# Both feed-forward projections of a residual block by one level of Strassen's seven block products

## The chip, the cores and the metric

The kernel runs on one core of a Trainium2 chip. The time is the device time of one execution in microseconds; the kernel before takes 2693.98 us (median of three runs, 2692.53 to 2694.37). The engines are TensorE (PE, with its weight loads as PEld), VectorE (DVE), ScalarE (ACT), GpSimd (POOL) and SyncE (SP), which issues the DMAs here.

## The reference

One residual block over 2048 rows of 1024 float32 numbers: a mixer (a gated linear recurrence beside stick-breaking attention) and a feed-forward part, which is where the change is:

```python
def rms_norm(x, g):
    xf = x.astype(jnp.float32)
    xf = xf * lax.rsqrt(jnp.mean(xf * xf, axis=-1, keepdims=True) + EPS)
    return xf.astype(x.dtype) * g
...
        x = x + jnp.einsum('bse,ed->bsd', y, w_out[l])

        h2 = rms_norm(x, norm_ffn[l])
        gu = jnp.einsum('bsd,df->bsf', h2, w_ffn_in[l])
        x = x + jnp.einsum('bsf,fd->bsd', jax.nn.silu(gu[..., :D_FF]) * gu[..., D_FF:], w_ffn_out[l])
    return rms_norm(x, norm_final)
```

D_FF is 2816, 22 tiles of 128. The two projections are 2048 x 1024 x 5632 and 2048 x 2816 x 1024.

## The kernel before

**Products in three parts.** Each float32 operand is split into a high part rounded to fp32r (an ACT cast) and the low rest (a subtraction on DVE or POOL). A product is three matmuls, high by high, high by low and low by high (`mm3`, lines 115 to 118), which add up in one PSUM bank of 128x512.

**The order.** The PE order is the order in which the program is written. The other engines' instructions are placed by a scheduler at build time, and each engine runs its list strictly in order; an instruction at the head of a list that waits holds all behind it.

**The mixer** goes through four groups (`NG`) of 512 rows. The projections of the next group, and in the last group the products with `w_out` (`Mix.run`, PSUM `po`), are fill between the steps of attention. `store_rows` writes the finished rows to DRAM (`x2_d`) and takes their norms. The products of the last group's attention branch come after all attention (`tail.run`).

**Feed-forward.** It takes two halves of 1024 rows. `make_h2` loads rows back (`hn`), scales them, transposes them on PE (`h2t`) and splits them (`hhi`, `hlo`), 16 tiles of 128x512 for a half. `gate_up` then takes one tile f of D_FF at a time: weights `gur`, 512 KB for gate (j = 0) and up (j = 1) each, split into `guh` and `gul`, and 8 steps of the contraction for two token groups into the banks `pgu`. SiLU on ACT (L829), the product with up on DVE (L830) and a split into `ahi` and `alo` keep the result on chip. After every two tiles `down` multiplies what the previous two left with `dnr`, split into `dnh` and `dnl`, into 16 banks `pw`; DVE adds each at once to the rows in SBUF (L860). So the two projections alternate all the way. At the end of a half `finish` takes the final norm: squares on ACT (L884), a product with the gain `gfin` on POOL (L888), a Newton reciprocal root of small DVE instructions, a scaling and a store.

Of the kernel before, what the change touches and what calls it, by code (L numbers as in the profile page):

```python
# [36 lines left out]
FCH = 2  # L37
# [11 lines left out]
HB = 8  # L49
# half groups of mixer weights loaded ahead, and held before their parts are kept in DRAM  # L50
# [3 lines left out]
# units of filling before the first branch's product, and fewer of them in the last group  # L54
# [3 lines left out]
# the last row tiles of the groups in which the final norm is taken  # L58
ENDS = (2, 4, 6, 7)
# [7 lines left out]
def tile_block(ctx: ExitStack, tc: tile.TileContext, x, w_in, w_out, w_gu, w_dn,  # L67
# [72 lines left out]
    def load_x(g, parts=1):  # L140
        """The normalized rows of a token group, before the gain, in pieces."""
# [40 lines left out]
    def load_half(src, name, key, keep):  # L182
        """Half (over k) of a group of weight columns, split; the parts are kept in DRAM for the next use."""
# [52 lines left out]
    def proj_col(g, cg, c, w, use, mid=None):  # L236
        """A transposed column tile of group cg; use(column tile, psum) evacuates."""
# [50 lines left out]
    # ---- attention  # L288
# [28 lines left out]
    def score(p, s):  # L317
# [10 lines left out]
        # u is what each key leaves to the older ones, 1 - beta  # L328
# [18 lines left out]
    def turn(p, s):  # L347
        """Transposes the weights of a query tile and splits them."""
# [339 lines left out]
    with tc.manual_schedule(engines={mybir.EngineType.PE}):  # L688
# [112 lines left out]
        for _ in h2:  # L801
            pass
# [173 lines left out]
```

## Time and profile before

| | |
|---|---|
| median of three runs | 2693.98 us |
| span of the profiled execution | 7685.8 us |
| matmuls and transposes in the span | 13472 |
| PE, DVE, ACT, POOL busy | 7656.3, 1421.4, 1124.6, 896.9 us |
| moved by DMA | 350.05 MB |

The profiled execution took 2.85 times as long as a run without the profiler. 2693.98 us over 13472 matmuls and transposes are 0.200 us each, 7685.8 over the same are 0.570: the profile's steps on PE can't be those of the run. What the trace shows for PE is its order and its counts. Its durations on the other engines and of transfers have nothing to do with PE's step, and are used as they stand.

### The profile page before, as it was taken

The page shows a single profiled execution, that of the slowest core. Times are in us where ns is not written, and L with a number is a line of the kernel's source. Part 1 is how long each engine was busy: PE and PEld are TensorE (multiplying, and loading weights), DVE is VectorE, ACT ScalarE, POOL GpSimd, SP SyncE. Part 2 cuts the span into 40 slices and gives each one's busy share as a digit, 9 for nine tenths or more (in the row PEclk, how much of TensorE's full clock was granted, in tenths as well). Part 3 has the DMA queues.
Part 4 walks back from the last instruction along what each step waited for, and adds up shares of the span by engine and source line. Part 5 has one row for each costly group of instructions (what it writes and reads, how often), then busy time and mean ns, then how long its engine had stood idle before and what let it go on. Part 6 is the DMA issues. An engine that isn't in the chain of part 4 may idle for free.

```text
span 7685.8 us, 36652 instructions
## 1 busy us (share of the span) xinstructions
PE 7656.3 (100%) x13472; PEld 5024.0 (65%) x13472; DVE 1421.4 (18%) x2278; ACT 1124.6 (15%) x2024; POOL 896.9 (12%) x1261
## 2 busy tenths in 40 slices
PE   9999999999999999999999999999999999999999
PEld 5665676767676888888755555555555555555555
DVE  1112222223333333333100000000011000000002
ACT  2112212222222222222100000000011000000001
POOL 2211101100001110000010111111111111111111
DMA  3222222121111222211200000000011000000000
GB/s 106 78 82 73 92 71 69 59 71 55 56 59 61 68 76 66 76 50 49 79 19 14 19 19 18 18 19 19 17 36 55 19 19 17 19 19 19 17 17 25
DMA packets 167445, 350.05 MB, mean 46 GB/s; under 512 B 17504, under 2 KB 58464, under 8 KB 167264
## 3 DMA queue, kind: packets, MB, share of 16 engines
q1 hardware_dynamic: 167264, 347.70, 13.7%
q8 instruction: 106, 1.74, 0.1%
q14 instruction: 75, 0.61, 0.0%
HBM read 268.20 MB, written 79.43 MB: 45 GB/s over the span
## 4 chain that ended last, share of the span: by engine, by line
PE 100%; DVE 0%; DMA 0%; SPq 0%; issue 0%; ACT 0%
PE pgu L116 11%; PE pgu L117 11%; PE pgu L118 11%; PE y L375 6%; PE z L325 6%; PE t L360 6%; PE pw L117 6%; PE pw L116 5%; PE pj L116 5%; PE pj L118 5%; PE pw L118 5%; PE pj L117 5%; PE po L116 3%; PE po L117 3%; PE po L118 3%; PE pv L117 1%
## 5 line engine op out<-in xcount | busy, mean ns | idle before, releaser
L116 PE MATMUL pgu<-hhi,guh 128*128 128x512 f32 x1408 | 1201.0, 853 | 0.0
L117 PE MATMUL pgu<-hlo,guh 128*128 128x512 f32 x1408 | 1200.2, 852 | 0.0
L118 PE MATMUL pgu<-hhi,gul 128*128 128x512 f32 x1408 | 1200.1, 852 | 0.0
L116 PEld LDWEIGHTS pgu<-hhi,guh 128*128 128x128 f32 x1408 | 505.8, 359 | 363.1 <-issue 361.6
L117 PEld LDWEIGHTS pgu<-hlo,guh 128*128 128x128 f32 x1408 | 505.2, 359 | 360.6 <-issue 360.6
L118 PEld LDWEIGHTS pgu<-hhi,gul 128*128 128x128 f32 x1408 | 503.7, 358 | 362.9 <-issue 358.7
L116 PE MATMUL pj<-ht_hi,w_hi 128*128 128x512 f32 x512 | 601.0, 1174 | 0.0
L117 PE MATMUL pw<-dnl,ahi 128*128 128x512 f32 x704 | 587.9, 835 | 0.0
L118 PE MATMUL pw<-dnh,alo 128*128 128x512 f32 x704 | 587.6, 835 | 0.0
L116 PE MATMUL pw<-dnh,ahi 128*128 128x512 f32 x704 | 586.5, 833 | 0.0
L118 PE MATMUL pj<-ht_hi,w_lo 128*128 128x512 f32 x512 | 559.7, 1093 | 0.0
L117 PE MATMUL pj<-ht_lo,w_hi 128*128 128x512 f32 x512 | 559.0, 1092 | 0.0
L325 PE MATMUL z<-ks,qd 128*128 128x512 f32 (+2 forms) x640 | 552.6, 998 | 0.0
L360 PE MATMUL t<-ident,be 128*128 128x128 f32 x1088 | 534.3, 690 | 0.0
L830 DVE TENSOR_TENSOR sg<-pgu,sg 128x512 f32<-128x512 f32 x88 | 60.9, 692 | 2530.6 <-PE pgu L118 2516.7
L860 DVE TENSOR_TENSOR x<-pw,x 128x512 f32<-128x512 f32 x352 | 243.4, 692 | 987.0 <-PE pw L118 987.0
L360 PEld LDWEIGHTS t<-ident,be 128*128 128x128 f32 x1088 | 270.8, 249 | 234.2 <-issue 160.4
L785 POOL TENSOR_TENSOR gul<-gur,guh 128x1024 fp32r<-128x1024 f32 x88 | 208.0, 2364 | 1729.8 <-ACT guh L784 1635.4
L375 PE MATMUL y<-al,vs 128*128 128x256 f32 x576 | 395.7, 687 | 0.0
L375 PE MATMUL y<-ah,vs 128*128 128x256 f32 x576 | 395.0, 686 | 0.0
L116 PE MATMUL po<-wo_hi,yhi 128*128 128x256 f32 x512 | 384.2, 750 | 0.0
L118 PEld LDWEIGHTS pw<-dnh,alo 128*128 128x128 f32 x704 | 249.6, 355 | 172.8 <-issue 172.4
(183 smaller groups left out, 7820.4 us busy)
## 6 DMA issues: line engine op xcount, KB each, us to landing
gur<-in_w_gu SPq DMA_DIRECT2D x88, 512.0 KB, 3.4
w_hi<-w_d SPq DMA_DIRECT2D x50, 512.0 KB, 3.3
w_lo<-w_d SPq DMA_DIRECT2D x50, 512.0 KB, 4.6
dnr<-in_w_dn SPq DMA_DIRECT2D x88, 256.0 KB, 2.6
vs<-vs_d SPq DMA_DIRECT2D x80, 256.0 KB, 3.0
ks<-ks_d SPq DMA_DIRECT2D x80, 256.0 KB, 3.0
qd<-q_d SPq DMA_DIRECT2D x128, 128.0 KB, 2.8
w_raw<-in_w_in SPq DMA_DIRECT2D x30, 512.0 KB, 4.3
```

Of the source, the lines that this page charges most:

```text
L116: nc.tensor.matmul(ps, lhsT=w_hi, rhs=m_hi, start=first, stop=False)
L117: nc.tensor.matmul(ps, lhsT=w_hi, rhs=m_lo, start=False, stop=False)
L118: nc.tensor.matmul(ps, lhsT=w_lo, rhs=m_hi, start=False, stop=last)
L325: nc.tensor.matmul(z[:, :nz], lhsT=qd[:, i, qs], rhs=kss[p.c][:, :nz], start=i == 0, stop=i == 1)
L360: nc.tensor.transpose(tp[:, b, :], p.be[s][:, b * P:(b + 1) * P], ident)
L375: nc.tensor.matmul(y, lhsT=vs[:, b, :], rhs=t[:, b].rearrange("p s q -> p (s q)"), start=first and m == 0, stop=last and m == 1)
L785: nc.gpsimd.tensor_tensor(out=wlo, in0=raw, in1=f32(whi), op=ALU.subtract)
L830: nc.vector.tensor_tensor(out=sg, in0=pss[1, g], in1=sg, op=ALU.mult)
L860: nc.vector.tensor_tensor(out=x2[t][:, ns], in0=ps, in1=x2[t][:, ns], op=ALU.add)
```

## The change

**Gate-up.** Two tiles of D_FF, two halves of the contraction and two token groups form a 2x2 by 2x2 block product, a "quad" (`quad`). It had 8 block products of 12 matmuls (4 steps of the contraction, three parts); now it has 7. Weights are combined for each quad (`prep_weights`: s1 to s4), tokens once for a half (`prep_tokens`: t1 to t4). There are 44 quads: gate, then up, for 11 pairs of tiles in each half. The result goes to DRAM (`act_d`), 11.5 MB for a half.

**Down** is a stage of its own, after all of gate-up. For each half it takes seven products one after another (0 to 6 here), and each goes through the contraction in six chunks: five of two tiles (24 matmuls), and a last one of one tile (12). `operands` makes a chunk's two operands, one chunk ahead (`bp`, two buffers): a sum or difference `sa` of results on POOL, one `sb` of weights on DVE (in place, so it bears the name `dr`), a cast of each on ACT, the low parts on DVE (`blo`, and `alo` where there is a `sa`) or POOL. Products 0 and 3 have `sa` alone, 1 and 2 `sb` alone, 4 to 6 both. At the end of a product `add` puts each of four banks into one to three places of the rows. `finish` for most of the final norm is called after product 5, the rest in product 6.

**The rows for feed-forward.** `turn_rows` scales, transposes and evacuates a finished token group and writes it to DRAM (`h2_d`); for groups 0 to 2 this is fill in the last group's attention, for group 3 it follows the last product with `w_out`. `prep_tokens` loads tiles of `h2_d` and makes the combinations.

```diff
...
+ORDER = (("a11", "b11"), ("s3", "t3"), ("s2", "t2"), ("s1", "t1"), ("a22", "t4"), ("s4", "b22"), ("a12", "b21"))
+EARLY = ("b11", "t1", "t2", "t3", "t4")
...
+DOWN = (
...
+    (((0, 0, 1), (1, 1, 1)), ((0, 0, 1), (1, 1, 1)), ((0, 0, 1), (1, 1, 1))),
+    (((1, 0, 1), (0, 0, -1)), ((0, 0, 1), (0, 1, 1)), ((1, 1, 1),)),
+    (((0, 1, 1), (1, 1, -1)), ((1, 0, 1), (1, 1, 1)), ((0, 0, 1),)),
+)
+CHUNKS = ((0, 2), (4, 2), (8, 2), (12, 2), (16, 2), (20, 1))
...
+    def turn_rows(g, x2):
...
+        for k in range(KD):
+            tp = ps_d.tile([P, GT], F32, tag="d", name=f"h2t{g}_{k}")
+            for t in range(TPG):
+                nc.tensor.transpose(tp[:, t * P:(t + 1) * P], x2[t][:, k * P:(k + 1) * P], ident)
+            ht = stg.tile([P, GT], F32, tag="s", name=f"h2{g}_{k}")
+            nc.scalar.activation(ht, tp, AF.Copy, scale=gf[:, k:k + 1])
+            nc.sync.dma_start(out=h2_d[g][k], in_=ht)
...
+            def split(q, kk, src, pool):
+                hi, lo = (t[:, kk] for t in tok[q])
+                nc.scalar.copy(hi, src)
+                (nc.gpsimd if pool else nc.vector).tensor_tensor(out=lo, in0=src, in1=f32(hi), op=ALU.subtract)
...
+                    b11, b12, b22 = load(0, 0), load(0, 1), load(1, 1)
+                    split("b11", kk, b11, True)
+                    t3 = prp.tile([P, GT], F32, tag="r", name=f"t3_{half}_{kk}")
+                    nc.vector.tensor_tensor(out=t3, in0=b22, in1=b12, op=ALU.subtract)
...
+        steps = prep_tokens(0, EARLY)
+            if i % 3 == 2:
+                next(steps, None)
+        for _ in turn_rows(NG - 1, tail_x2):
+            next(steps, None)
+        for _ in steps:
...
+            hi = wsp.tile([P, KD, P], F32R, tag="hi2", name=f"a1h{nm}", bufs=2)
+            lo = wsp.tile([P, KD, P], F32R, tag="lo2", name=f"a1l{nm}", bufs=2)
+            nc.scalar.copy(hi, r[0])
+            nc.gpsimd.tensor_tensor(out=lo, in0=r[0], in1=f32(hi), op=ALU.subtract)
+            w["a11"], w["a12"] = (hi[:, :K2], lo[:, :K2]), (hi[:, K2:], lo[:, K2:])
+            s3 = new("s3", a11, a21, ALU.subtract)
+            split("s3", s3, True)
+            s1 = new("s1", a21, a22, ALU.add)
+            s2 = new("s2", s1, a11, ALU.subtract)
+            split("s2", s2, False)
+            split("s1", s1, False)
+            split("a22", a22, True)
+            nc.vector.tensor_tensor(out=s2, in0=a12, in1=s2, op=ALU.subtract)
+            split("s4", s2, True)
...
+            product("a", 0)
+            p1 = keep("a", "p1")
+            product("c", 1)
+            product("a", 2, True)
+            u2 = keep("a", "u2")
+            u3 = tmp.tile([P, GT], F32, tag="t", name=f"u3{nm}")
+            nc.vector.tensor_tensor(out=u3, in0=ps["c"], in1=u2, op=ALU.add)
+            product("d", 3)
+            use(1, 1, ps["d"], u3)
+            product("c", 4, True)
+            use(1, 0, ps["c"], u2)
+            product("d", 5, True)
+            use(0, 1, ps["d"], u2)
+            product("b", 6)
+            use(0, 0, ps["b"], p1)
...
+            def use(i, k, ps, part):
+                c = tmp.tile([P, GT], F32, tag="c", name=f"c{half}_{fp}_{j}_{i}{k}", bufs=CB)
+                nc.vector.tensor_tensor(out=c, in0=ps, in1=part, op=ALU.add)
+                if j == 0:
+                    nc.scalar.activation(c, c, AF.Silu)
+                    gates[i, k] = c
+                else:
+                    nc.vector.tensor_tensor(out=c, in0=c, in1=gates[i, k], op=ALU.mult)
+                    nc.sync.dma_start(out=act_d[half][2 * fp + i][:, k], in_=c)
...
+                r0 = (f0 + j * m) * P
+                nc.sync.dma_start(out=t, in_=w_dn[r0:r0 + m * P, k * GT:(k + 1) * GT].rearrange("(m p) c -> p m c", p=P))
+                bb.append(t)
+            sa = aa[0]
+            if len(ta) == 2:
+                sa = bp.tile([P, m, GT], F32, tag="sa", name=f"sa{nm}")
+                nc.gpsimd.tensor_tensor(out=sa, in0=aa[0], in1=aa[1], op=ALU.add if ta[1][2] > 0 else ALU.subtract)
+            sb = bb[0]
+            if len(tb) == 2:
+                nc.vector.tensor_tensor(out=sb, in0=bb[0], in1=bb[1], op=ALU.add if tb[1][2] > 0 else ALU.subtract)
+            out = []
+            for q, src, eng in (("a", sa, nc.gpsimd if len(ta) == 1 else nc.vector), ("b", sb, nc.vector)):
+                hi = bp.tile([P, m, GT], F32R, tag=f"{q}hi", name=f"{q}hi{nm}")
+                lo = bp.tile([P, m, GT], F32R, tag=f"{q}lo", name=f"{q}lo{nm}")
+                nc.scalar.copy(hi, src)
+                eng.tensor_tensor(out=lo, in0=src, in1=f32(hi), op=ALU.subtract)
+                out.append((hi, lo))
+            return out
...
+        def add(half, p, t, ps):
+            x2 = rows(half)
+            for i, k, sign in DOWN[p][2]:
+                xs = x2[i * TPG + t][:, k * GT:(k + 1) * GT]
+                if sign > 0:
+                    nc.vector.tensor_tensor(out=xs, in0=ps, in1=xs, op=ALU.add)
+                else:
...
+                    sq = op.tile([P, GT], F32, tag="sq", name=f"sqo{half}_{t}_{c}", bufs=1)
+                    nc.scalar.activation(sq, x2[t][:, cs], AF.Square, accum_out=ss[:, t, c:c + 1])
+                    o = os[t, c] = op.tile([P, GT], F32, tag="o", name=f"o{half}_{t}_{c}")
+                    if (t, c) != (TPG - 1, 0):
+                        nc.gpsimd.tensor_tensor(out=o, in0=x2[t][:, cs], in1=gfin[:, cs], op=ALU.mult)
...
+            if last and p == len(DOWN) - 2:
+                for t in range(TPG, TPH):
+                    finish(half, t, 1, ss, os, (0, 1))
+                    if t % 2:
+                        write(half, t - 1, 2, ss, os)
+                finish(half, 0, TPG, ss, os, (1,))
```

How it shifts the engines' lists shows at five places. First DVE in gate-up of the kernel before, some 40 us of feed-forward (sg is SiLU of gate, x2 the rows, pw a bank of the down product):

```order
L830 TENSOR_TENSOR sg0_6_0_16883<-pgu0_6_1_0_16833,sg0_6_0_16883 128x512
L830 TENSOR_TENSOR sg0_6_1_16890<-pgu0_6_1_1_16858,sg0_6_1_16890 128x512
L830 TENSOR_TENSOR sg0_7_0_17009<-pgu0_7_1_0_16959,sg0_7_0_17009 128x512
L830 TENSOR_TENSOR sg0_7_1_17016<-pgu0_7_1_1_16984,sg0_7_1_17016 128x512
L860 TENSOR_TENSOR x2_0_0_15707<-pw0_4_0_0_17035,x2_0_0_15707 128x512
L860 TENSOR_TENSOR x2_0_1_15709<-pw0_4_1_0_17043,x2_0_1_15709 128x512
```

The same engine in a quad of the changed kernel (s2l and s1l are low parts of the next quad's weights, u3 a partial sum out of bank c, c the results):

```order
L862 TENSOR_TENSOR s2l0_1_0_16209<-s2s0_1_0_16206,s2h0_1_0_16208 128x512
L882 TENSOR_TENSOR s2s0_1_0_16206<-r0_1_0_0_16190,s2s0_1_0_16206 128x512
L862 TENSOR_TENSOR s1l0_1_0_16213<-s1s0_1_0_16204,s1h0_1_0_16212 128x512
L907 TENSOR_TENSOR u30_0_1_16269<-psc0_0_1_16227,u20_0_1_16267 128x512
L934 TENSOR_TENSOR c0_0_1_11_16283<-psd0_0_1_16228,u30_0_1_16269 128x512
L939 TENSOR_TENSOR c0_0_1_11_16283<-c0_0_1_11_16283,c0_0_0_11_16142 128x512
L934 TENSOR_TENSOR c0_0_1_10_16299<-psc0_0_1_16227,u20_0_1_16267 128x512
L939 TENSOR_TENSOR c0_0_1_10_16299<-c0_0_1_10_16299,c0_0_0_10_16157 128x512
```

DVE reads PSUM in every row of before; now the weight rows have both inputs in SBUF, and u3, which must be out of bank c before product 4 of the quad may add to it, stands behind s1l.

DVE at the boundary of products 4 and 5 of the down stage (names end in half_product_chunk; dr with two inputs is sb):

```order
L1002 TENSOR_TENSOR blo0_4_3_23485<-dr0_4_3_00_23473,bhi0_4_3_23484 128x1024
L996 TENSOR_TENSOR dr0_4_4_00_23512<-dr0_4_4_00_23512,dr0_4_4_11_23514 128x1024
L996 TENSOR_TENSOR dr0_4_5_00_23551<-dr0_4_5_00_23551,dr0_4_5_11_23553 128x512
L1002 TENSOR_TENSOR alo0_4_4_23520<-sa0_4_4_23516,ahi0_4_4_23519 128x1024
L1002 TENSOR_TENSOR blo0_4_4_23524<-dr0_4_4_00_23512,bhi0_4_4_23523 128x1024
L996 TENSOR_TENSOR dr0_5_0_00_23590<-dr0_5_0_00_23590,dr0_5_0_01_23592 128x1024
L1002 TENSOR_TENSOR alo0_4_5_23559<-sa0_4_5_23555,ahi0_4_5_23558 128x512
L1002 TENSOR_TENSOR blo0_4_5_23563<-dr0_4_5_00_23551,bhi0_4_5_23562 128x512
L996 TENSOR_TENSOR dr0_5_1_00_23625<-dr0_5_1_00_23625,dr0_5_1_01_23627 128x1024
L1011 TENSOR_TENSOR x2_0_0_22489<-pw0_4_0_23406,x2_0_0_22489 128x512
L1002 TENSOR_TENSOR alo0_5_0_23598<-sa0_5_0_23594,ahi0_5_0_23597 128x1024
```

The sum for chunk 5 stands ahead of the low parts of chunk 4, so it waits for its weights in front of them; and the first addition to the rows stands ahead of chunk 0's low parts of the next product.

POOL in product 6 of the first half (sa are sums of results, o the rows times the final gain):

```order
L993 TENSOR_TENSOR sa0_6_0_23828<-act0_0_22455 128x1024
L993 TENSOR_TENSOR sa0_6_1_23977<-act0_1_22472 128x1024
L1025 TENSOR_TENSOR o0_4_1_23861<-x2_0_4_22497,gfin_22453 128x512
L1025 TENSOR_TENSOR o0_5_0_23865<-x2_0_5_22499,gfin_22453 128x512
L993 TENSOR_TENSOR sa0_6_2_24020<-act0_2_22534 128x1024
L1025 TENSOR_TENSOR o0_5_1_23869<-x2_0_5_22499,gfin_22453 128x512
L1025 TENSOR_TENSOR o0_6_0_23908<-x2_0_6_22501,gfin_22453 128x512
L1025 TENSOR_TENSOR o0_6_1_23912<-x2_0_6_22501,gfin_22453 128x512
L1025 TENSOR_TENSOR o0_7_0_23916<-x2_0_7_22503,gfin_22453 128x512
L1025 TENSOR_TENSOR o0_7_1_23920<-x2_0_7_22503,gfin_22453 128x512
L993 TENSOR_TENSOR sa0_6_3_24059<-act0_3_22575 128x1024
```

Ten products o stand between the sums of chunks 1 and 5, seven of them here; the sum of chunk 3 comes after these seven.

SP where gate-up of both halves ends and down begins (c are the last results of gate-up, act and x2 the loads of down):

```order
L940 DMA act_d1_20_191<-c1_10_1_00_22424 128x512
L988 DMA dr0_0_1_00_22477<-in_w_dn 128x2x512
L973 DMA x2_0_2_22493<-x2_d0_113 128x1024
L964 DMA act0_0_22455<-act_d0_0_149 128x1024
L964 DMA act0_0_22455<-act_d0_1_150 128x1024
L964 DMA act0_0_22455<-act_d0_2_151 128x1024
L964 DMA act0_0_22455<-act_d0_3_152 128x1024
L964 DMA act0_1_22472<-act_d0_4_153 128x1024
L964 DMA act0_1_22472<-act_d0_5_154 128x1024
L964 DMA act0_1_22472<-act_d0_6_155 128x1024
L964 DMA act0_1_22472<-act_d0_7_156 128x1024
L973 DMA x2_0_3_22495<-x2_d0_113 128x1024
```

Down's loads of results stand behind the last store of gate-up; before, nothing was loaded there but weights.

## Rows read from the trace of the kernel before

**Rows 1.** Page, head and busy time of PE.

```profile
span 7685.8 us, 36652 instructions
PE 7656.3 (100%) x13472; PEld 5024.0 (65%) x13472; DVE 1421.4 (18%) x2278; ACT 1124.6 (15%) x2024; POOL 896.9 (12%) x1261
```

**Rows 2.** Page, the chain that ended last, by engine.

```profile
PE 100%; DVE 0%; DMA 0%; SPq 0%; issue 0%; ACT 0%
```

**Rows 3.** Windows: the mixer, all of feed-forward, and a stretch of it.

```profile
core 0: us, PE busy (x) PEld busy (x) DVE busy (x) ACT busy (x) POOL busy (x), PEclk, DMA share, GB/s
0.00:4000.00 4000.00, 3980.46 (x7330) 2859.25 (x7331) 1075.29 (x1694) 845.86 (x1594) 458.06 (x983) 1.00 0.21 68
4000.00:7686.00 3686.00, 3675.89 (x6143) 2164.77 (x6141) 346.08 (x584) 278.71 (x430) 438.80 (x278) 1.00 0.06 21
...
4600.00:5200.00 600.00, 600.00 (x1009) 354.55 (x1009) 53.98 (x78) 38.77 (x55) 69.25 (x44) 1.00 0.06 19
```

**Rows 4.** Lines: matmuls of gate-up and down (one of three each).

```profile
L116 PE MATMUL pgu<-hhi,guh 128*128 128x512 f32 x1408 | 1201.0, 853 | 0.0
L118 PE MATMUL pw<-dnh,alo 128*128 128x512 f32 x704 | 587.6, 835 | 0.0
```

**Rows 5.** Lines of ACT: casts, copies, evacuation, squares (busy us, mean ns).

```profile
L784 ACT CAST guh<-gur 128x1024 fp32r<-128x1024 f32 x88 | 92.0, 1047 | 1065.6 <-PE pgu L117 1063.0 <-DMA gur<-in_w_gu 2.6
L844 ACT CAST dnh<-dnr 128x512 fp32r<-128x512 f32 x88 | 54.2, 619 | 1089.6 <-PE pw L118 1089.6
L775 ACT ACTIVATE hhi<-h2t,gf 128x512 fp32r<-128x512 f32 x32 | 22.0, 687 | 53.1 <-PE h2t L774 53.1
L520 ACT COPY gx<-pj 128x512 f32<-128x512 f32 x16 | 9.4, 586 | 63.4 <-PE pj L118 63.4
```

**Rows 6.** Lines of DVE, forms apart.

```profile
L860 DVE TENSOR_TENSOR x<-pw,x 128x512 f32<-128x512 f32 x352 | 243.4, 692 | 987.0 <-PE pw L118 987.0
L776 DVE SCALAR_TENSOR_TENSOR hlo<-h2t,gf,hhi 128x512 fp32r<-128x512 f32 x32 | 24.0, 751 | 44.3 <-ACT hhi L775 44.3
L362 DVE TENSOR_TENSOR al<-t,ah 128x384 fp32r<-128x384 f32 x32 | 17.9, 558 | 128.7 <-ACT ah L361 128.7
L362 DVE TENSOR_TENSOR al<-t,ah 128x128 fp32r<-128x128 f32 x32 | 9.3, 291 | 120.0 <-ACT ah L361 120.0
```

**Rows 7.** Lines of POOL.

```profile
L785 POOL TENSOR_TENSOR gul<-gur,guh 128x1024 fp32r<-128x1024 f32 x88 | 208.0, 2364 | 1729.8 <-ACT guh L784 1635.4 <-DMA x_d<-xo 94.4
L888 POOL TENSOR_TENSOR o<-x,gfin 128x512 f32<-128x512 f32 x30 | 37.9, 1276 | 84.4 <-DVE x L860 25.4 <-PE h2t L774 21.6 <-DMA out<-o 16.9
```

**Rows 8.** DMA: KB of one, median us to landing.

```profile
w_lo<-w_d SPq DMA_DIRECT2D x50, 512.0 KB, 4.6
hn<-x_d SPq DMA_DIRECT2D x32, 256.0 KB, 3.9
```

**Rows 9.** Windows at the start, where loads queue up.

```profile
0.00:5.00 5.00, 0.00 (x0) 0.00 (x0) 0.41 (x5) 1.87 (x3) 1.41 (x14) 1.00 0.59 210
5.00:10.00 5.00, 0.00 (x0) 0.00 (x0) 2.55 (x15) 4.75 (x17) 0.00 (x0) 1.00 1.03 377
```

**Rows 10.** Timeline: DVE and POOL side by side (start us, us).

```profile
3566.96 1.31 POOL L613 TENSOR_TENSOR acc<-acc,yt 128x512 f32<-128x512 f32 x1 [8.31 <-ACT yt L612]
3567.06 2.29 DVE L339 TENSOR_TENSOR_SCAN u<-u,u,zero 128x513 f32<-128x513 f32 x1
...
3569.94 0.68 DVE L345 TENSOR_TENSOR be<-be,u 128x512 f32<-128x512 f32 x1
3569.97 1.78 POOL L613 TENSOR_TENSOR acc<-acc,yt 128x512 f32<-128x512 f32 x1 [0.46 <-ACT yt L612]
```

**Rows 11.** Lines of DVE: the same scan, mean of all.

```profile
L339 DVE TENSOR_TENSOR_SCAN u<-u,u,zero 128x513 f32<-128x513 f32 x192 | 249.9, 1302 | 501.9 <-ACT u L329 501.6 <-POOL u L327 0.2
```

**Rows 12.** The chain at the end of the span.

```profile
7675.40 0.50 PE pw L118
7675.93 0.69 DVE x L860
...
7680.68 0.72 ACT o L904
```

More of the change, by code (lines that the diff above doesn't have):

```diff
@@ L48 @@
 WB = 4
-HB = 8
+WSB = 6
+CB = 6
+OB = 8
 AHEAD = 2
@@ L85, in tile_block @@
     x2_d = [dram.tile([GT, D], F32, name=f"x2_d{i}") for i in range(NG)]
+    h2_d = [[dram.tile([P, GT], F32, name=f"h2_d{i}_{k}") for k in range(KD)] for i in range(NG)]
+    act_d = [[dram.tile([P, 2, GT], F32, name=f"act_d{i}_{f}") for f in range(NF)] for i in range(NHALF)]
     smp = ctx.enter_context(tc.tile_pool(name="smp", bufs=2))
@@ L780, in split_gu @@
-        def split_gu(raw, half, f, j):
-            nc.sync.dma_start(out=raw, in_=w_gu[f, j])
-            whi = wgu.tile([P, KD, P], F32R, tag="gu_hi", name=f"guh{half}_{f}_{j}")
-            wlo = wgu.tile([P, KD, P], F32R, tag="gu_lo", name=f"gul{half}_{f}_{j}")
-            nc.scalar.copy(whi, raw)
-            nc.gpsimd.tensor_tensor(out=wlo, in0=raw, in1=f32(whi), op=ALU.subtract)
-            return whi, wlo
-        early = {}
-        h2 = make_h2(0)
-        hs = next(h2)
-        for _ in range(KD):
-            next(h2)
+        up_r = ExitStack()
@@ new lines, in tile_block, with act, rows @@
+        acts, x2s = {}, {}
+        def act(half, c):
+            if (half, c) not in acts:
+                f0, m = CHUNKS[c]
+                t = acts[half, c] = actp.tile([P, 2 * m, 2, GT], F32, tag=f"act{c}", name=f"act{half}_{c}")
+                for i in range(2 * m):
+                    nc.sync.dma_start(out=t[:, i], in_=act_d[half][f0 + i])
+            return acts[half, c]
+        def rows(half):
+            if half not in x2s:
+                x2s[half] = []
+                for t in range(TPH):
+                    xt = x2p.tile([P, D], F32, tag=f"x2_{t}", name=f"x2_{half}_{t}")
+                    gt = half * TPH + t
+                    nc.sync.dma_start(out=xt, in_=x2_d[gt // TPG][gt % TPG * P:(gt % TPG + 1) * P, :])
+                    x2s[half].append(xt)
+            return x2s[half]
@@ new lines, in tile_block @@
+        work = [(half, p, c) for half in range(NHALF) for p in range(len(DOWN)) for c in range(len(CHUNKS))]
+        ready = operands(*work[0])
+        pss = {}
+        for n, (half, p, c) in enumerate(work):
+            (ahi, alo), (bhi, blo) = ready
+            if n + 1 < len(work):
+                ready = operands(*work[n + 1])
+            if c == 0:
+                rows(half)
+                if p == 0:
+                    ss = smp.tile([P, TPH, 2], F32, tag="sso", name=f"sso{half}", bufs=1)
+                    os = {}
+            last = c == len(CHUNKS) - 1
+            for t in range(TPG):
+                if c == 0:
+                    pss[t] = ps_w.tile([P, GT], F32, tag="w", name=f"pw{half}_{p}_{t}")
+                ts = slice(t * P, (t + 1) * P)
+                m = CHUNKS[c][1]
+                for i in range(m):
+                    mm3(pss[t], ahi[:, i, ts], alo[:, i, ts], bhi[:, i], blo[:, i],
+                        c == 0 and i == 0, last and i == m - 1)
+                if not last:
+                    continue
+                add(half, p, t, pss[t])
+                if p == len(DOWN) - 1:
+                    finish(half, t, 1, ss, os, (0,))
+                    if t >= TPG - 2:
+                        write(half, *((0, TPG - 1) if t == TPG - 2 else (t, 1)), ss, os)
+            if last and p == len(DOWN) - 2:
+                for t in range(TPG, TPH):
+                    finish(half, t, 1, ss, os, (0, 1))
+                    if t % 2:
+                        write(half, t - 1, 2, ss, os)
+                finish(half, 0, TPG, ss, os, (1,))
```

286 lines of the change are left out of this document (134 added, 152 removed), and 4 rows, old and new, of the table DOWN.

## The prediction

> **What bounds the kernel now.** I read the page's head first, then the chain, then windows. In the profiled execution PE is busy 100% of the span and the chain is PE alone [rows 1, 2]. That tells little of the run: in a stretch of feed-forward 1009 matmuls take 600 us, 0.595 us each [rows 3], and 13472 at the run's mean take 0.200. So the profile hides under PE whatever doesn't exceed 0.6 us per matmul, and PE's duration must be bounded otherwise. A matmul of 512 columns at the granted clock (1.00 in every window, the level of 2.4 GHz) takes no less than 0.213 us. From above: DVE is busy 1075 us before 4000 us [rows 3], its durations hold in the run, so the mixer takes at least 1075 us of the 2694, and the 6143 matmuls behind it at most 0.263 each. I take 0.22, near the floor, since in feed-forward no other engine comes near PE's load: DVE's 346 us, POOL's 439 and ACT's 279 [rows 3] stand against 6143 x 0.213 = 1310 us. So feed-forward is bound by PE in the run too, and fewer matmuls shorten it.
>
> The Trainium skill (TensorE: Matmul & The Clock Gate, Wait — 56ns, not 53.3ns?) gives 215.7 ns from one warm matmul of 512 columns to the next. By that the gain below would be 171 us instead of 174; no row here shows it, the profile's step is 0.595.
>
> **What goes.** Gate-up has 3 x 1408 matmuls and down 3 x 704 [rows 4], 6336 in all. After: 44 quads x 84 = 3696, and 14 products x (5 x 24 + 12) = 1848; 5544. It saves 792 x 0.22 = 174 us (169 by the floor, 208 by the ceiling).
>
> **What comes, gate-up.** A product of a quad lasts 12 x 0.22 = 2.64 us, a quad 18.5. For each quad DVE has eight instructions with both inputs in SBUF and five that read PSUM, 0.69 each [rows 6], 9.0 us; POOL 2.36 + 3 x 1.28 = 6.2 [rows 7]; ACT one cast of 1.05, five of 0.62 and two copies of 0.59 [rows 5], 5.3, and SiLU every other quad. All fit in 18.5. The tight place is u3: after the third product ACT casts s1h (0.62) and copies u2 (0.59), DVE adds u3 (0.69): 1.9 us and some hand-offs, against the 2.64 of product 3, which goes to another bank. It fits with some 0.4 us to spare, so I cost it at nothing; a rival says what it costs when the cover is gone.
>
> **What comes, around the stages.** (a) Three groups' 96 transposes, 24 evacuations and 12 row scalings lie in the last attention, where the 32 transposes of half of `make_h2` had been in the tail: 24 x 0.69 [rows 5] = 17 us of ACT beside work on PE, 0 to 10 on the path, 6 taken. (b) Group 3: after the last `po` the root, scalings, eight evacuations (5.5) and a store and load through DRAM (each some 4 us [rows 8]) stand ahead of gate-up, about 14 us where before about 8 were; 5 to 14 more, I take 8. (c) Between halves the kernel before is paced by 16 evacuations of `h2t`, 16 x 0.75 = 12 us on DVE [rows 6]. After, eight tile pairs of combinations wait for buffers that the last products hold; the ones that the first product needs take about 15 us, 23 if DVE and POOL take turns. 4 to 13 more, 8 taken. (d) From gate-up to down: SP's list puts the loads of results behind the last store, so the first product needs 0.5 (gain) + 4.2 (rows) + 11.5 (results) + 2.9 (weights) = 19.1 MB while it runs. At 377 GB/s, the highest of the rows [rows 9], that is 51 us, and some 5 more until the last chunk is prepared and multiplied: 56 where 132 x 0.22 = 29 us of work are. 27 lost; at 210 GB/s [rows 9] it is 67. (e) Between the halves of down the next results come behind the output's stores, partly under product 6: 12 us (5 to 20).
> These are 6 + 8 + 8 + 27 + 12 = 61 us, with 41 and 107 as ends.
>
> **What comes, in down's chunks.** A chunk of two tiles lasts 24 x 0.22 = 5.28 us on PE, a product 29. An operation of 128x1024 takes POOL 2.36 [rows 7], ACT 1.05 [rows 5]; for DVE no row has it, and I go on from 384 and 128 columns, 558 and 291 ns [rows 6], 134 ns for each 128: 1.23. DVE has 2.5 us in a chunk of products 0 to 3 and 3.7 in one of 4 to 6, POOL 2.36, ACT 2.1: less than 5.28. A pair of weight loads lands in 4.6 [rows 8]; with issue, sum, cast and low part, some 9 us, under the 10.6 of the two chunks for which the buffers hold. So within a product nothing stalls if the engines work side by side. At each boundary it does: the last chunk gives PE only 2.64 us of cover, and the eight additions to the rows (8 x 0.69 [rows 6] = 5.5 us) get between the preparations of the next. From the order at products 4 and 5 I get 1 to 3 us for each of 14 boundaries, 29 together (14 to 42).
>
> **DVE and POOL beside each other.** Nearly everything that is added has both inputs in SBUF, and there the trace speaks against the change. A scan of 1.30 us [rows 11] takes 2.29 when it starts 0.10 us after a POOL sum of 1.31: of 1.21 us side by side 0.99 are lost. The other way, POOL's 1.28 becomes 1.78 beside a DVE product of two SBUF inputs, 0.50 of 0.65 [rows 10, 7]. So about 80% of the time side by side is paid by whoever comes second. In products 4 to 6 a chunk then needs 3 x 1.23 + 2.36 = 6.0 us instead of 5.28: with the boundaries some 7 us a product for 4 and 5 that weren't in the sum above. Product 6 has ten `o` of 1.28 [rows 7] among POOL's sums besides: 13 + 13 of POOL and 20 of DVE make 46 us against 29, 17 lost. Products 1 to 3 lose about 2 each: (7 + 4.5 + 17 + 6) x 2 halves = 69; less what is already at the boundaries, 52, and at 80% of it 42. If it costs nothing, 0 and 2 to 4 us for `finish`.
> The Trainium skill (SBUF — State Buffer, Who interferes with whom) says that a VectorE instruction with two SBUF inputs and a GpSimd one that reads SBUF exclude each other for the whole instruction, and that one with an input in PSUM doesn't. The rows agree on the first (80%, not all of it). By its full exclusion the sum below would be 10 us higher, 2662.
>
> **Sum.** -174 + 61 + 29 + 42 = -42 us: 2694 - 42 = 2652. The end doesn't change: some 10 us from the last matmul [rows 12, 1]. Against the profile's own span PE saves 792 x 0.595 = 471 us there, products last 2.7 times as long and cover chunks and u3; some 60 us of transitions are left: 7685.8 - 471 + 60 = 7275 us.
>
> **Rivals.**
> A, the forecast: DVE and POOL take turns as in the rows: 2652 (2635 to 2675).
> B: they hardly meet, because POOL's sums run one chunk ahead, while DVE waits for weights; for it speaks that a chunk's work is 60 to 70% of 5.28 us for each of them. The 42 fall away: 2610. With loads of the first product better spread, or with PE at 0.25 us per matmul (198 saved), 2585 to 2590.
> C, slower than before: u3 comes late. In the DVE list it stands behind s1l, which has both inputs in SBUF. If POOL's low part of 128x1024 (2.36 us [rows 7]) runs just then, s1l starts up to 2.36 later and u3 ends 1.9 + 2.36 - 2.64 and hand-offs, about 1.8 us, after product 3; PE waits, 44 times: 79 us, 2731. It decides from 42/44 = 0.95 us per quad on. Against it: that POOL instruction is released by the cast a1h, which waits for the last product of a quad, and should be done 4 us before. The same sign comes if down's loads go at 210 GB/s: 109 MB take 520 us, the 407 of PE with all of the stalls above, and (d) grows by 40: 2692 or more.
> D: the gain is only spent: the ends of the losses, 107 + 42 + 42 = 191 us, against 174 saved give 2711, so a point between, at 132 + 42, gives no change: about 2694.
>
> **Chances.** A 0.47, B 0.27, C 0.18, D 0.08. About 0.2%, 5 us, can be told from no change. Faster are A, B: 0.74 and a little of D; same 0.07; slower C and the rest of D, 0.18. The range reaches from 2585 (B) to 2718, where it leaves out the upper part of C and what is below B.
>
> **What would show it.** In the changed profile: 5544 matmuls of 128x512 in feed-forward. (a) to (e): windows at the four transitions where PE isn't busy, the longest at gate-up to down, with DMA near 377 GB/s. DVE low parts `alo`, `blo` above 1.23 us and POOL's `sa` above 2.36 where they overlap; in product 6 PE's weight loads released by DVE `alo` behind POOL `o`. In gate-up no wait of PE for u3. I am wrong if `psc` matmuls wait for DVE's L907 in most quads (C), if `sa` and `blo` keep 2.36 and 1.23 side by side (B), or if loads for chunks land later than 9 us.

## The result and the profile after

The changed kernel takes 2724.02 us (median of four runs, 2721.45 to 2726.95) against 2693.32 for the kernel before on the same chip: ratio 1.0112, 95% interval 1.0098 to 1.0127, 31 us slower. The prediction was 2652, faster with a chance of 0.75; its range ended at 2718.

The profile of the changed kernel runs at the run's own pace, which that of the kernel before didn't [rows 1]. Its head, the busy times, and the clock in 40 slices (tenths of full speed):

```profile
span 2722.9 us, 36800 instructions
PE 2443.0 (90%) x12680; PEld 2049.7 (75%) x12680; DVE 1983.9 (73%) x2730; ACT 1308.0 (48%) x2328; POOL 1040.4 (38%) x1285
PEclk9999999999999998998999999899999889988998
```

PE has 792 matmuls and transposes fewer (12680 against 13472), and DVE is at 73% of the span. Windows of the changed kernel by stage: mixer up to the last product with `w_out`, way into gate-up, gate-up, hand-over, down, end:

```profile
core 0: us, PE busy (x) PEld busy (x) DVE busy (x) ACT busy (x) POOL busy (x), PEclk, DMA share, GB/s
0.00:1250.30 1250.30, 1118.54 (x7103) 987.25 (x7104) 1060.00 (x1680) 804.60 (x1589) 443.25 (x975) 0.97 0.64 211
1250.30:1268.90 18.60, 6.67 (x35) 5.33 (x33) 9.37 (x24) 11.59 (x22) 4.97 (x3) 0.72 0.67 234
1268.90:2156.30 887.40, 861.56 (x3696) 695.39 (x3696) 512.10 (x596) 301.67 (x472) 310.26 (x194) 0.99 0.25 84
2156.30:2175.20 18.90, 0.18 (x2) 0.01 (x1) 3.86 (x5) 3.13 (x3) 2.34 (x1) 0.57 0.96 360
2175.20:2709.80 534.60, 455.87 (x1848) 361.71 (x1848) 391.40 (x393) 182.49 (x236) 276.85 (x111) 0.92 0.53 188
2709.80:2723.00 13.20, 0.17 (x1) 0.00 (x0) 7.21 (x34) 4.48 (x10) 2.74 (x3) 0.71 0.41 159
```

To set this beside the kernel before, its stages were needed at the same pace. That is the first experiment.

### The profile page after: what moved, and what is told of

Its sections match the earlier page's. It is cut to its first block, busy times and chain, and to the rows that moved or that the text cites. A ratio compares the mean times of both kernels' runs of the same rounds, so it can differ in the third digit from the quotient of the medians.

```text
span 2722.9 us, 36800 instructions
## 1 busy us (share of the span) xinstructions
PE 2443.0 (90%) x12680; PEld 2049.7 (75%) x12680; DVE 1983.9 (73%) x2730; ACT 1308.0 (48%) x2328; POOL 1040.4 (38%) x1285
## 5 line engine op out<-in xcount | busy, mean ns | idle before, releaser
L135 PE MATMUL pw<-blo,ahi 128*128 128x512 f32 x616 | 255.0, 414 | 55.7 <-DVE blo L1002 55.7
L134 PE MATMUL pw<-bhi,ahi 128*128 128x512 f32 x616 | 249.4, 405 | 41.7 <-ACT bhi L1001 23.0
L357 DVE TENSOR_TENSOR_SCAN u<-u,u,zero 128x513 f32<-128x513 f32 x192 | 254.7, 1328 | 18.9 <-ACT u L347 18.4
L136 PE MATMUL pw<-bhi,alo 128*128 128x512 f32 x616 | 249.6, 405 | 0.0
L378 PE MATMUL t<-ident,be 128*128 128x128 f32 x1088 | 177.6, 279 | 49.4 <-DVE al L380 44.5
L134 PE MATMUL pj<-ht_hi,w_hi 128*128 128x512 f32 x512 | 214.7, 419 | 2.3 <-DVE sl L276 1.5
L136 PE MATMUL pj<-ht_hi,w_lo 128*128 128x512 f32 x512 | 201.6, 394 | 0.0
L135 PE MATMUL pj<-ht_lo,w_hi 128*128 128x512 f32 x512 | 201.3, 393 | 0.0
L343 PE MATMUL z<-ks,qd 128*128 128x512 f32 (+2 forms) x640 | 189.4, 377 | 8.2 <-ACT be L348 6.6
L393 PE MATMUL y<-ah,vs 128*128 128x256 f32 x576 | 150.0, 291 | 10.9 <-DVE yp L403 10.7
```

The costliest lines, as they stand in the source:

```text
L343: nc.tensor.matmul(z[:, :nz], lhsT=qd[:, i, qs], rhs=kss[p.c][:, :nz], start=i == 0, stop=i == 1)
L357: nc.vector.tensor_tensor_scan(out=ur, data0=ur, data1=zero.broadcast_to([P, n + 1]), initial=1.0 if p.prev is None else p.prev.u[s][:, 0: ...
L378: nc.tensor.transpose(tp[:, b, :], p.be[s][:, b * P:(b + 1) * P], ident)
```

## Experiments

**The kernel before once more** (e1). No edit.

> The kernel before, unchanged, profiled once more, to have its stages at the run's pace, which its first profile hid. The changed kernel's profile shows 0.2266 us per 128x512 matmul in down and 0.2317 in gate-up. If that pace holds here, feed-forward's 6336 matmuls take 1436 to 1468 us, its transition between halves about 12, and the mixer ends near 1220 to 1245 us, against 1269 at the first quad of the changed kernel. If the mixer ends at 1260 or later, the change costs nothing there and all of the loss is in feed-forward.

2695.86 us, and this time the profile kept the run's pace. Windows: mixer up to its last product with `w_out`, feed-forward, end (columns as above):

```profile
0.00:1221.10 1221.10, 1110.96 (x7072) 974.97 (x7073) 1045.06 (x1674) 792.02 (x1571) 440.24 (x969) 0.99 0.64 214
1221.10:2675.10 1454.00, 1450.09 (x6402) 1197.74 (x6400) 346.72 (x556) 286.25 (x440) 461.96 (x288) 1.00 0.18 60
2675.10:2694.10 19.00, 0.16 (x1) 0.00 (x0) 13.94 (x49) 6.28 (x13) 5.36 (x5) 0.62 0.37 138
```

From one start to the next, a feed-forward matmul takes 0.2266 us in the kernel before, in gate-up and in down (the commonest steps in the trace are 226 and 227 ns). 6336 of them are 1436 of the 1454 us: feed-forward ran with 18 us lost. Now 5544 at 0.2266 are 1256, but from the first gate-up matmul to the last of down it is 887.4 + 18.9 + 534.6 = 1440.9 us: 185 are lost. Of the 179 us that the change removes, 166 come back in feed-forward (184.6 - 18.3), and 48 are added ahead of it (29.2 in the mixer, 18.6 on the way in); the end is 5.8 shorter. 166 + 48 - 179 - 6 = 29, the difference of the spans, 2722.9 - 2694.1 = 28.8.

The way into gate-up needs a second look. In the kernel before, gate-up follows the last product with `w_out` at once (timeline of PE in this run, start, us):

```profile
1221.02 0.28 PE L118 MATMUL po<-wo_hi,ylo 128*128 128x256 f32 x1
1221.14 0.39 PE L116 MATMUL pgu<-hhi,guh 128*128 128x512 f32 x1
```

Its 64 transposes `h2t` for the first half stand between the last products, at 1183.6 to 1203.8 us, and are done by then.

**Which of the two projections pays, and what the stages cost.** The down table with ordinary products (e2; the first two of eight lines):

```diff
 DOWN = (
+    (((1, 0, 1),), ((0, 0, 1),), ((1, 0, 1),)),
+    (((1, 1, 1),), ((1, 0, 1),), ((1, 0, 1),)),
...
```

> The changed kernel with the down stage's seven products replaced by the ordinary eight (table of products alone; stages, chunks and traffic through DRAM stay). 264 matmuls more are 60 us. Theory S (the stages cost it: loads at the start of each half, the final norm in the last product): the stalls of product 0 and of the last one stay, some 75 us of the 116 in down, and small ones at 16 starts come to 25, so the time rises by 45 to 60 us, to 2765 to 2785. Theory X (DVE and POOL exclude each other in the sums): the sums are gone, so most of the 116 us go and the time is 2700 to 2730, no worse than the seven products.

Gate-up with ordinary products (e3):

```diff
+            for n, (bank, i, k) in enumerate((("a", 0, 0), ("b", 0, 1), ("c", 1, 0), ("d", 1, 1))):
+                for m in range(2):
+                    wq, tq = ORDER[2 * n + m]
...
+                use(i, k, ps[bank])
```

> The changed kernel with the ordinary eight products in gate-up (96 matmuls a quad instead of 84; no combinations of weights or tokens; stages and DRAM traffic stay). 528 matmuls more at 0.2317 are 122 us. Theory S: the quads of the changed kernel hide their combinations (19.5 us each, 84 x 0.2317), so all of the 122 come back less some 10 us of the transition between halves: 2825 to 2850. Theory X: combinations on DVE and POOL slow the quads, so the ordinary form gives some back: 2800 or less.

Both with ordinary products (e4):

> Both with the ordinary eight products, in the changed kernel's stages: as many feed-forward matmuls as the kernel before, so the difference to it is what the stages and the way through DRAM cost. Theory S: 2860 to 2900, some 170 to 200 us over before, more than the 179 that 792 matmuls save. Theory X: the stages are nearly free, 2700 to 2760.

| gate-up | down | us | over the kernel before, ratio and interval |
|---|---|---|---|
| seven | seven | 2724.0 | 1.0112 (1.0098 to 1.0127) |
| seven | eight | 2736.5 | 1.0156 (1.0140 to 1.0171) |
| eight | seven | 2835.8 | 1.0522 (1.0504 to 1.0540) |
| eight | eight | 2847.9 | 1.0568 (1.0552 to 1.0584) |

With ordinary products in both, the stages cost 2847.9 - 2695.0 = 153 us over the kernel before, without one matmul saved. In them gate-up's seven products give 112 us of the 122 that 528 matmuls are worth (at 0.2317 us each), down's give 12 of 60. Theory X fell for gate-up; for the stages S was nearer, its lowest figure, 170, was 17 us too high. For down neither was right: the eight products without sums (2736.5, below S's 2765 and above X's 2730) cost only 12 us more than the seven, so most of what the seven save is lost again. The stalls of down say where. With eight products they are 70.8 us, with seven 115.8. Of the 45 more, 41 are in the last two products of each half: 27.9 and 23.3 us with sums, 5.2 and 5.2 without, though POOL has the same 30 products with the final gain in both.

The 153 us of the stages (151 by the spans of the two profiles) add up from the trace of e4: 28 in the mixer, 18 on the way into gate-up, 28 in gate-up's quads (44 x (22.40 - 21.75), see below), 13 in the first quad and the one at the change of half, 16 from gate-up to down, 72 in down's products; against them stand the 18 that feed-forward lost before and an end that is 6 shorter.

**The way into gate-up.** Three gaps of 9.7 to 10.5 us stand in the fill of the last attention, where PE waits for DVE's scaling of a group's rows ahead of their transposes. Waits of the changed kernel between 890 and 1160 us (us in total, times, longest):

```profile
PE h2t L696 <- DVE xo L692: 29.6, 3, 10.2
```

First `turn_rows` was moved back (e5):

```diff
                 store_rows(g, x2)
+                for _ in range(TURN):
+                    yield
                 yield from turn_rows(g, x2)
```

> In the fill of the last attention, 8 units of other work stand between the rows of a group and their transposes, for the three groups, so that the norm is ready when PE comes to them; the changed kernel's profile has three gaps of 10 us there, and the kernel before reaches its last product with w_out 29 us earlier. Theory P (PE's fixed order costs the wait): the gaps shrink to under 3 us and 20 to 28 us come back, 2697 to 2704. Theory V (DVE, 95% busy there, is the bound, and the gaps only show its delay): the gaps go, other waits take their place, 2715 to 2724.

2721.02 (1.0102, 1.0087 to 1.0117): 3 us, which the intervals can't tell from nothing, with gaps of 8.5, 5.6 and 6.6. `TURN` is 8; each `yield` lets one unit of other work in between. Then the scaling was left out for groups 0 to 2 (e10, `if g < NG - 1: continue` at the head of its loop):

> The rows of groups 0 to 2 are transposed without their scaling by the root (left out: this scaling, 12 instructions), so the transposes in the fill of the last attention wait for no norm. Moving them 8 units back gave 3 us. Theory P (PE's wait for the norm is the loss in the mixer): the three gaps of 10 us go, and 20 to 28 us come back, 2696 to 2704. Theory V (DVE binds the last attention; the gaps on PE only take what it would wait for DVE anyway): 3 to 8 us, 2716 to 2721.

2702.17 (1.0028, 1.0017 to 1.0039): 22 us came back; the mixer's last product stands at 1228.2 us instead of 1250.3, and two gaps of 2.5 and 3.5 us are left. That is P's number, but the edit took work away as well as the wait, and the rows go on without their norm. The work is small: for three groups 6 scalings of 0.75 us on DVE and 6 of 1.14 on ACT, 11 us if nothing ran beside them. So at least some half of the 22 us is the wait. Then all work was kept, and `turn_rows` of groups 0 and 1 moved into the next group's products (e12):

> All work is done, but the transposes of groups 0 and 1 are held back into the next group's products (12 units after their start, one tile of four transposes every third unit), when their norm is long ready; the rows of group 1 lie in other buffers so that they can stay. Group 2 stays as it was. Leaving the scaling out gave back 22 us for three groups. Theory P (PE's wait for the norm): two of three gaps go, 12 to 16 us come back, 2708 to 2713. Theory V (the 22 us were the scaling's work on DVE and ACT, which binds there): 0 to 5 us, 2719 to 2726.

2722.06 (1.0111, 1.0097 to 1.0125), nothing. But the trace still shows PE waiting for the scaling, 8.0 us for group 1: the scaling had been moved along with the transposes. The last try was meant to delay the transposes alone (e14):

```diff
                 nc.vector.tensor_scalar(out=x2[t], in0=x2[t], scalar1=r, scalar2=None, op0=ALU.mult)
+        for _ in range(TURN if g < NG - 1 else 0):
+            yield
```

> The earlier delays held back the scaling together with the transposes, so each time DVE's scaling still stood right ahead of the transposes that wait for it. Here the scaling is issued at once after the rows' norm, and 8 units of other work stand between it and the transposes, for groups 0 to 2. Theory P (PE's wait for scaling that comes out of DVE's backlog): the three gaps of 10 us fall to under 3, and 15 to 22 us come back, 2702 to 2709. Theory V (the scaling's work itself): 0 to 5 us, 2719 to 2724.

2717.37 (1.0087, 1.0073 to 1.0101), 7 us, between the theories. But the edit didn't reach DVE: in the two traces PE and POOL have the same lists as in e5, and in DVE's the root still stands right ahead of the scaling. PE's waits between 890 and 1160 us are the same too, 10 us less than in the changed kernel (first e5, then this run):

```profile
PE h2t L697 <- DVE xo L693: 19.7, 3, 8.2
PE h2t L699 <- DVE xo L693: 19.7, 3, 8.3
```

So the two runs measure one thing, 3 and 7 us for 10 us less of gap, and this one decides nothing between P and V. Eight units last too little: in the trace of group 0 PE stops at 906.2, and the scaling starts at 913.6, after a root of some twelve dependent DVE steps of 0.2 us with attention's work between them. What speaks for the wait is e10, 22 us for 24 us less of gap, and that the three gaps, 29.6 us, are as long as the mixer's whole loss. How much of e10's 22 us is the scaling's work stays open within the bound above.

**Gate-up's step.** Quads of the changed kernel show no wait, but take 19.47 us, where 84 x 0.2266 = 19.03. Windows of one quad, first five products and last two (60 and 24 matmuls by the weight loads):

```profile
1467.87:1481.87 14.00, 14.00 (x61) 11.27 (x60) 7.73 (x9) 4.59 (x7) 4.47 (x3) 1.00 0.20 75
1481.87:1487.34 5.47, 5.47 (x26) 4.51 (x24) 3.75 (x5) 2.54 (x5) 2.59 (x2) 1.00 0.29 99
```

That is 0.2333 us a step, then 0.228. A shift of the tokens in SBUF by 32 bytes was tried (e6, a tile of 128x8 ahead of the pool `prp`):

> A tile of 32 bytes ahead of the pools on the right side of SBUF moves the tokens of gate-up by 32 bytes; nothing else changes. In the changed kernel five of a quad's seven products, whose tokens start at addresses that are 32 beyond a multiple of 64 while their weights start at multiples of 64, step by 0.2325 us, and the two whose tokens start at multiples of 64 by 0.2266; in the kernel before both were 32 beyond, and it stepped by 0.2266. Theory A (the offset between the two): all quads step by 0.2266, 19.0 us instead of 19.5, and 15 to 20 us come back, 2704 to 2709. Theory B (the place of the pool, or the amount of other traffic): no change, 2724.

2724.03 (1.0115, 1.0100 to 1.0130): no change, theory A fell. Then the weights (e9):

```diff
-        wsp = uctx.enter_context(tc.tile_pool(name="wsp", bufs=WSB, side="left"))
+        wsp = uctx.enter_context(tc.tile_pool(name="wsp", bufs=WSB, side="right"))
```

> The split weights of gate-up move from the left to the right side of SBUF, where five of a quad's seven token operands are; nothing else changes. In the changed kernel matmuls with weights on the left and tokens on the right step by 0.2325 us, with both on the left (last two products, and all of down) by 0.2266, and in the kernel before with both on the right by 0.2266. The 32 byte shift left them at 0.2335. Theory H (weights and tokens on different sides step slower): now the first five products step by 0.2266 and the last two by 0.2325; a quad takes 19.2 us instead of 19.5, and 9 to 13 us come back: 2711 to 2715. Theory T (another cause, such as which tokens or how much traffic): no change, 2724.

The same two windows with the weights on the right:

```profile
1474.58:1488.22 13.64, 13.64 (x62) 11.27 (x60) 7.67 (x9) 4.59 (x7) 4.36 (x3) 1.00 0.20 77
1488.22:1493.82 5.60, 5.60 (x25) 4.50 (x24) 3.71 (x5) 2.54 (x5) 2.61 (x2) 1.00 0.30 97
```

Now the first five step by 0.2273 and the last two by 0.2333: theory H, to the product. e4 agrees: there all tokens of gate-up are on the right and all weights on the left, and a quad of 96 matmuls takes 22.40 us, 0.2333 each. A quad of e9 is 0.23 us shorter, 10 us in 44. The time stayed, 2726.13 (1.0118, 1.0102 to 1.0133): gate-up starts at 1272.8 instead of 1268.9, and its first quad takes 28.6 instead of 23.7, probably since the weights now wait for buffers that the mixer holds; that wasn't tried.

**Product 6 and the final gain.** The stalls of down by product, from the starts of the matmuls in the trace of the changed kernel (length less 132 x 0.2266):

| product | 0 | 1 | 2 | 3 | 4 | 5 | 6 |
|---|---|---|---|---|---|---|---|
| first half, us | 11.6 | 8.9 | 2.2 | 2.1 | 2.9 | 4.7 | 23.2 |
| second half, us | 21.9 | 7.8 | 2.2 | 2.1 | 2.9 | 4.8 | 18.5 |

Product 6 of the first half, timeline of DVE and POOL (start, us):

```profile
2396.76 9.39 POOL L1025 TENSOR_TENSOR o<-x,gfin 128x512 f32<-128x512 f32 x5
2397.82 1.24 DVE L1030 TENSOR_TENSOR ssp<-sso 128x2 f32<-128x2 f32 x1
2398.99 1.21 DVE L1002 TENSOR_TENSOR blo<-dr,bhi 128x1024 fp32r<-128x1024 f32 x1
2400.12 1.26 DVE L109 TENSOR_SCALAR ro_v<-ssp 128x2 f32<-128x2 f32 x1
2401.29 1.22 DVE L996 TENSOR_TENSOR dr<-dr,dr 128x1024 f32<-128x1024 f32 x1
2402.43 1.26 DVE L111 TENSOR_SCALAR ro_t<-ro_v 128x2 int32<-128x2 int32 x1
2403.60 0.15 DVE L1030 TENSOR_TENSOR ssp<-sso 128x2 f32<-128x2 f32 x1
2403.72 1.22 DVE L113 TENSOR_SCALAR ro_y<-ro_t 128x2 int32<-128x2 int32 x1
```

DVE and POOL take strict turns: an instruction on 128x2 numbers, 0.15 us by itself, takes 1.2 while POOL has a product, and POOL's five take 1.88 each instead of 1.28 [rows 7]. The chunk's low part `blo` and the next sum `dr` stand in this queue, and PE waits for them (waits between 2387 and 2440 us):

```profile
PE pw L135 <- DVE blo L1002: 17.1, 3, 8.3
```

The product with the gain went from POOL to one DVE instruction (e7):

```diff
-                    if (t, c) != (TPG - 1, 0):
-                        nc.gpsimd.tensor_tensor(out=o, in0=x2[t][:, cs], in1=gfin[:, cs], op=ALU.mult)
...
+                    nc.vector.scalar_tensor_tensor(out=os[t, c], in0=x2[t][:, cs], scalar=r, in1=gfin[:, cs],
+                                                   op0=ALU.mult, op1=ALU.mult)
```

> The product with the final gain leaves POOL: one DVE instruction does root, row and gain at once, as the last tile does already, in place of 15 POOL products and a scaling on ACT or DVE for each half. Theory X (POOL's products and DVE exclude each other): in product 6 of down DVE's instructions on 128x4 numbers take 1.1 to 2.3 us instead of 0.16 while POOL has its products; they go back to 0.16, the stalls of product 6, 23.2 and 18.5 us, fall to 5 to 10, and the time to 2695 to 2705. Theory Q (the length of DVE's queue): 12 instructions of 0.75 are added to the same queue, the stalls stay above 15, 2715 to 2730.

2701.84 (1.0031, 1.0020 to 1.0042): 22 us came back though DVE got more work, and product 6 loses 10.4 and 8.2 us. In the timeline of this run most of the small instructions are back to 0.16, and some that meet a `sa` still aren't:

```profile
2395.25 3.37 POOL L993 TENSOR_TENSOR sa<-act 128x1024 f32<-128x1024 f32 x1 [1.16 <-DVE ssp L1027]
2396.30 2.35 DVE L109 TENSOR_SCALAR ro_v<-ssp 128x2 f32<-128x2 f32 x1
2398.57 1.22 DVE L996 TENSOR_TENSOR dr<-dr,dr 128x1024 f32<-128x1024 f32 x1
2399.70 0.16 DVE L111 TENSOR_SCALAR ro_t<-ro_v 128x2 int32<-128x2 int32 x1
```

Theory X holds. The Trainium skill (SBUF — State Buffer, Who interferes with whom) says that the one which comes second waits until the other is done, and that `tensor_scalar` may be among those that do. The two L109 rows agree, with 1.26 and 2.35 us on 128x2 numbers: the second ends when the `sa` of 3.37 us does, at 2398.6. The change needs both, the sums and the gain on POOL: without sums (e2) the gain stayed on POOL, and the last product of a half lost 1.9 us.

**The loads of product 0** (e8).

```diff
-            if c == 0:
+            if c == len(CHUNKS) - 2:
                 rows(half)
+            if c == 0:
```

> The rows of a half (4.2 MB) are asked for at chunk 4 of product 0 instead of ahead of it, so that six of eight stand behind the loads of results in SP's list. 4.2 MB at 377 GB/s are 11 us. Theory L (the loads of the first product bind, in the order of SP's list): 8 to 11 us come back in the first half, and in the second half, where the rows stand behind the stores of the output, 8 to 16 of the 21.9 us: 2698 to 2708. Theory M (the last results of gate-up and the hand-over bind): within 4 us of 2724.

2717.20 (1.0095, 1.0078 to 1.0113): 7 us, with an interval that overlaps that of the changed kernel, 1.0098 to 1.0127; the stalls are clearer. Products 0 and 1 of the first half lose 12.8 us instead of 20.5, of the second 25.5 instead of 29.7; the hand-over stays at 18.7. Theory L, with its size below the low end: the second half hardly gained, and its product 0 not at all (22.6 us). There SP's list holds it. The first half's stores of the output wait at its head for DVE, and the next weights stand behind them (waits of SP in this run between 2420 and 2465 us):

```profile
SPq L1043 <- DVE o L1042: 16.1, 1, 16.1
```

Whether product 0 gains when these stores are moved wasn't tried.

**Together.** Gain on DVE, rows later, weights on the right, scaling on ACT and 16 units ahead of `turn_rows` (e11):

> What helped, together: the final gain on DVE (22 us measured alone), the rows asked for later (7), 16 units of other work ahead of the transposes in the mixer with the row scalings of groups 0 to 2 on ACT (3 or more), and the weights of gate-up on the right (0 by theory T, 9 to 13 by theory H). If the parts add up, 2724 - 22 - 7 - 4 - (0 to 11) = 2680 to 2691, 3 to 14 us below the kernel before; if rows and gain give back the same stall in product 0 of the second half, 2685 to 2696.

2707.44 (1.0041, 1.0029 to 1.0054), no better than the gain alone (1.0020 to 1.0042): the mixer's last product came at 1259.7 us, 9 later than in the changed kernel, and the first quad took 28.3. Without the last three of these, and with `turn_rows` of groups 0 and 1 in the next group's products (e13):

> The same, with the final gain on DVE (22 us measured alone) and the rows asked for later (7). By theory P 2724 - 22 - 7 - 14 = 2681, and with what rows and gain share in product 0 of the second half up to 2688: 0.2 to 0.5% below the kernel before. By theory V 2692 to 2698, level with it.

2691.10 (0.9988, 0.9979 to 0.9997). With the eight units ahead of the transposes instead (e15):

> The same, with the final gain on DVE (22 us measured alone) and the rows asked for later (7). By theory P 2675 to 2683, 0.4 to 0.7% below the kernel before; by theory V 2690 to 2697, level with it.

2687.58 (0.9974, 0.9965 to 0.9983), 0.26% below the kernel before. Its down stage by the windows (columns as above), where the changed kernel had 534.6:

```profile
2173.90:2678.30 504.40, 449.21 (x1848) 356.45 (x1848) 377.19 (x405) 175.29 (x224) 229.22 (x83) 0.95 0.56 199
```

## Why the prediction was wrong

| step, as the prediction named it | said | measured |
|---|---|---|
| What goes | -174 | -179 |
| (a) the three groups in the fill of attention | 6 | 29 |
| (b) group 3, way into gate-up | 8 | 18.6 |
| gate-up's quads, costed at nothing | 0 | 19 |
| (c) between halves | 8 | 13 |
| (d) from gate-up to down | 27 | 30.5 |
| (e) between the halves of down | 12 | 22 |
| down's chunks, boundaries and taking turns | 29 + 42 | 82 |
| the end | 0 | -6 |
| sum | -42 | 29 |

Measured: (a), (b) and the end from the windows of the two profiles; quads 44 x (19.47 - 19.03); (c) the quad at the change of half, 46.0 - 19.5, and the first one, 23.7 - 19.5, less the 18 us that feed-forward lost before; (d) 18.9 and product 0's 11.6; (e) product 0's 21.9; chunks all other products of down.

**The step that failed is (a)**, 6 us where 29 were measured, 23 of the 72 us by which the time was missed. It set 17 us of evacuations on ACT against work on PE and took 6. It priced what the moved work does on its own engine and not what PE must wait for: rows, norm, scaling, transposes are a chain through DVE, which is busy for 246.4 of the 270 us from 890 to 1160, and in PE's list the transposes stand right behind the rows. The list offers PE nothing else in the gap. The traces show the three gaps, 29.6 us; e10 shows that most of them go with the scaling, but no run took the wait away and kept all work.

**(b)** failed by what it credited to the kernel before. It took some 8 us there between the last product with `w_out` and gate-up, and (a) took 32 transposes in the tail; in e1 there are 64, and nothing lies between the two matmuls. After, 18.6 us are needed and not 14. Together (a) and (b) are 34 us too low.

**The sum of the ends.** The ends of (a) to (e), 10, 14, 13, 67 and 20, add up to 124 and not to 107. With 124 rival D's own worst case is 2728 instead of 2711, above the measured 2724. The five terms measured 113.

**Gate-up's quads** had no wait for u3 (waits of the changed kernel between 1300 and 2150 us):

```profile
PE psc L134 <- DVE u L907: 0.2, 1, 0.2
```

Rival C, the slower one, named the wrong mechanism: the time came out slower, but not by it. In the quad shown above the low part of 128x1024 on POOL was done 5.2 us before s1l, as its counter-argument said. That a matmul itself steps 3% slower with its operands on different sides of SBUF was in no term.

**Down.** (d) was right, as mechanism and size. (e) had the mechanism, results behind the output's stores, and 12 us where 22 were measured. Taking turns was right as mechanism, shown by e7, and rival B fell by the prediction's own sign: `sa` takes 3.02 us instead of 2.36, `blo` 1.54 instead of 1.23 (lines of the changed kernel, 2175 to 2710 us):

```profile
L993 POOL TENSOR_TENSOR sa<-act 128x1024 f32<-128x1024 f32 x49 | 147.9, 3019 | 139.2 <-DVE alo L1002 89.7 <-DMA act<-act_d 45.7 <-DVE ro_y L122 3.8
L1002 DVE TENSOR_TENSOR blo<-dr,bhi 128x1024 fp32r<-128x1024 f32 x68 | 104.4, 1538 | 14.8 <-ACT bhi L1001 14.3
```

So was its place, product 6; the size of the chunk term was 11 us low, and products 4 and 5, priced at some 7 us each, lost 2.9 and 4.7.

**The clock** was missing in (a), (c) and all terms of down, and the first profile couldn't show it: PE never stood idle there, and the granted clock was 1.00 in every window. After a gap in the changed kernel the granted clock is at the lower of its two levels, 1.2 GHz, for some us. Windows right behind the first gap in the mixer and behind a stall of product 0:

```profile
915.40:920.00 4.60, 4.24 (x16) 3.36 (x17) 1.71 (x3) 3.83 (x7) 0.00 (x0) 0.52 0.32 129
2193.00:2199.80 6.80, 6.06 (x14) 4.81 (x15) 2.93 (x3) 1.99 (x2) 2.37 (x1) 0.50 1.03 413
```

In the second the matmuls step by 0.427 us. In the feed-forward part of the changed kernel 109 do so; 109 x 0.2 = 22 us of the losses above are this and not waits. In the kernel before it is 4 matmuls.

The pace, 0.22 us from bounds of 0.213 and 0.263, was good: 0.2266.

## What to carry to other kernels

Here the stages that the fast product scheme needs cost 153 us before the first matmul was saved, most of it PE waiting, so cost such stages first, each as a chain through every engine that it passes. Where an instruction list is fixed, ask of moved work how long the engine with the fixed list waits for it, and not only how long it keeps its own engine busy: 17 us of evacuations were priced, and gaps of 29.6 us came. Read the order of the kernel before as closely as that of the changed one: the 8 us credited to it were not there. Don't lay a dependent chain of small DVE instructions and a run of POOL instructions over the same stretch: moving 30 POOL products to DVE made this kernel 22 us faster. And look into the trace whether an edit moved what it was to move: e5 and e14 turned out to be one experiment.

## What was not expected of the hardware

A 128x512 fp32r matmul steps by 0.2266 us when its weights and its moving operand come from pools on the same side of SBUF (in the changed kernel the last two products of a quad and all of down, both on the left; in e9 the first five, 0.2273 on average, both on the right), and by 0.2333 when they don't (the first five of a quad in the changed kernel, weights left and tokens right). Moving the weights swapped which products were slow (e9). What decides, and where the border is, wasn't tried.

The first profile of the kernel before took 2.85 times the run, the second 1.00 times, with the same program. Durations on DVE, ACT and POOL agreed in both (a scan 1.30 and 1.33 us), so what was read from them held; PE's steps there were of no use.
